# TensorE's work as a rolled loop, and GpSimd's drain in its own stream, in a gather, running-sum and projection kernel

## The chip, the cores and the metric

The kernel runs on one core of a Trainium2 chip. The metric is the device time of one execution in microseconds (us); five executions of the kernel before lay within 0.4% (356.56 to 357.88 us). A *run* below is one execution. The *span* is what the profile covers of the one execution it shows, and is 1.7 to 1.8 us shorter than that execution's time. Runs have a state: on the disturbed chip of two batches below the kernel before took 420 to 458 us at a granted TensorE clock of 0.88 to 0.98, where it takes 356 to 359 us at 0.99 on the others, and those are not compared with undisturbed ones. PSUM is the memory in which the kernel has TensorE write its products. The engines are TensorE (PE; PEld is its weight loads), VectorE (DVE), ScalarE (ACT), GpSimd (POOL) and SyncE (SP); a `q` behind the name is the engine's sequencer or queue.

## The reference, cut to what matters

```python
B, S, N, D = (16, 4096, 2048, 512)            # x: [B, S, D] f32, w: [D, D] f32, indices sorted
gathered = x[b_idx, indices, :]               # 2048 of 4096 rows of each batch
cs = np.cumsum(gathered, axis=1)              # running sum down the rows
return np.matmul(cs, w).astype(np.float32)    # [16, 2048, 512]
```

67 MB are read by gather and 67 MB written. There are 256 tiles of 128 rows, handled as 128 groups of two.

## The kernel before

The kernel gives each engine its own stream of instructions, and lets the streams meet in counting semaphores. `Lane.need` emits a wait only where that engine has not already waited for as much. These are the parts that the change and the argument touch:

```python
NG = 16; NH = 3; NA = 4; NB = 2; NC = 4; NO = 8; AH = 2     # buffers; AH groups of sums ahead
...
ctx.enter_context(tc.tile_critical(no_gpsimd_drain=False))  # L78: opens and closes the program
...
def gather(t):          # GpSimd: 128 rows of x by index, one DMA of 256 KB
    g, r = divmod(t, R)
    pool.need(s_c, g + 1 - NG // R)
    ...
    nc.gpsimd.indirect_dma_start(...).then_inc(s_g[t % NG], 16)   # 16 completions

def cast(g):            # ScalarE: both tiles of a group to fp16
    for t in range(R * g, R * g + R):
        act.need(s_g[t % NG], 16 * (t // NG + 1))
    act.need(s_a, R * (g - NH + 1))
    nc.scalar.copy(out=g16[g % NH][:], in_=g32[g % (NG // R)][:]).then_inc(s_c, 1)

def sums(t):            # TensorE: running sum inside a tile, with a triangular matrix
    g, r = divmod(t, R)
    pe.need(s_c, g + 1)
    pe.need(s_ut, 4)
    pe.need(s_d, t - NA + 1)
    for c in range(DC): mm = nc.tensor.matmul(out=pa[t % NA][:, c], ...)
    mm.then_inc(s_a, 1)

# carry(t): VectorE adds the last column of the tile before and writes fp16 into cst

def project(g, j):      # TensorE: running sums times w
    pe.need(s_wc, 1)
    pe.need(s_d, R * (g + 1))
    pe.need(s_e, g - NB + 1)
    for c in range(DC): mm = nc.tensor.matmul(out=pb[g % NB][:, j], ...)
    mm.then_inc(s_b, 1)

# drain(g): ScalarE copies pb to ob;  store(g): SyncE sends 512 KB to the output
...
for g in range(G):      # TensorE's order: sums of group g+2, then projection of group g
    for j in range(R):
        t = R * (g + AH) + j
        if t < T: sums(t)
        project(g, j)
```

"Drain" has two meanings here: `drain(g)` is ScalarE's copy out of PSUM, called the PSUM copy from here on. The other is the instruction DRAIN in GpSimd's stream, called the drain.

## Time and profile before

| | before |
|---|---|
| time, median of 3 runs | 357.12 us (356.56 to 357.59) |
| the profiled run, its span | 356.41 us, 354.6 us |
| gathers | 256, one each 1.25 us |
| bytes moved | 135.92 MB, mean 383 GB/s |

From the page of the kernel before come the busy times of the engines (share of the span, number of instructions), the queue that carries instruction blocks (packets, MB, share of the DMA engines' time), and the chain that ended last, by engine:

```profile
PE 301.8 (85%) x2050; PEld 149.2 (42%) x2050; DVE 178.1 (50%) x260; ACT 257.9 (73%) x258; POOL 243.7 (69%) x264
...
q8 instruction: 17, 0.28, 0.3%
...
POOL 50%; DMA 22%; issue 17%; PE 5%; ACT 3%; ACTq 0%; SPq 0%
```

TensorE is the busiest engine, but only 5% of the chain is its work. The gathers on GpSimd, the time between two of them ("issue") and the DMA behind them are 89%. So the 301.8 us of TensorE are mostly beside the path. In the same kernel, the view of the gathered tile gives the time from a gather's issue to its landing:

```profile
DMA to landing us min/median/max: 3.2/10.2/15.3
```

### The profile page before, as it was taken

Reading aid. Unit: us, or ns where it says so; the run is one execution under the profiler, and the core shown is the slowest. Engines: PE = TensorE matmul, PEld = TensorE weight load, DVE = VectorE, ACT = ScalarE, POOL = GpSimd, SP = SyncE. Lnnn points to the kernel's source line nnn. Section 1 sums busy time; section 2 is a strip of 40 time slices with the busy share of each in tenths; the row PEclk is TensorE's granted clock in tenths of the full one; section 3 lists DMA queues with packets and bytes.
Section 4 is the critical chain, followed back from the end, with each engine's and each line's share of the span. In section 5 each row is a group of like instructions: output and inputs, shape, how many; then the busy total and the mean of one; then the engine's idle time right before and its main releaser. Section 6 shows DMA issues by size and latency. Waiting matters only on the chain.

```text
span 354.6 us, 5833 instructions
## 1 busy us (share of the span) xinstructions
PE 301.8 (85%) x2050; PEld 149.2 (42%) x2050; DVE 178.1 (50%) x260; ACT 257.9 (73%) x258; POOL 243.7 (69%) x264
## 2 busy tenths in 40 slices
PE   0497799999899999899898988989989889898880
PEld 0253354444354444444444444444444444444440
DVE  1354465555555555555554554645555555555530
ACT  0776687787788787777777777877878778687760
POOL 6777777777777777777777777777777777774000
PEclk9999999999999999999999999999999999999995
DMA  6789999999999999999999999999999999999761
GB/s 222 224 241 384 409 410 401 415 411 418 412 417 416 415 414 415 413 416 416 415 415 414 414 413 413 411 417 415 413 417 413 416 413 414 412 415 414 293 244 74
DMA packets 40029, 135.92 MB, mean 383 GB/s; under 512 B 6465, under 2 KB 6721, under 8 KB 40001
## 3 DMA queue, kind: packets, MB, share of 16 engines
q0 software_dynamic: 20480, 67.13, 48.5%
q1 hardware_dynamic: 19520, 68.43, 47.8%
q8 instruction: 17, 0.28, 0.3%
q14 instruction: 12, 0.09, 0.1%
HBM read 68.42 MB, written 67.11 MB: 382 GB/s over the span
## 4 chain that ended last, share of the span: by engine, by line
POOL 50%; DMA 22%; issue 17%; PE 5%; ACT 3%; ACTq 0%; SPq 0%
POOL g L108 50%; DMA g<-in_x_dram,idxg 21%; PE pb L160 4%; ACT g L120 3%; PE pa L128 1%; ACT ob L172 1%; DMA idx_first<-in_indices_dram 1%; ACTq L23 0%; SPq L284 0%; SPq L78 0%
## 5 line engine op out<-in xcount | busy, mean ns | idle before, releaser
L108 POOL DMA_INDIRECT g<-in_x_dram,idxg x254 | 240.5, 947 | 77.4 <-issue 71.3
L160 PE MATMUL pb<-w,cst 128*128 128x512 f16 x1024 | 263.5, 381 | 0.0
L148 DVE TENSOR_TENSOR cst<-pa,cst 128x512 f16<-128x512 f32 x240 | 166.0, 692 | 138.1 <-PE pa L128 137.3
L120 ACT CAST g<-g 128x1024 f16<-128x1024 f32 x128 | 133.6, 1045 | 66.9 <-issue 32.2
L172 ACT COPY ob<-pb 128x1024 f32<-128x1024 f32 x128 | 129.2, 1010 | 11.4 <-PE pb L160 9.8
L128 PE MATMUL pa<-ut,g 128*128 128x128 f16 x1024 | 101.1, 222 | 38.5 <-ACT g L120 37.8
L128 PEld LDWEIGHTS pa<-ut,g 128*128 128x128 f16 x1024 | 69.4, 99 | 128.4 <-ACT g L120 97.6
L160 PEld LDWEIGHTS pb<-w,cst 128*128 128x128 f16 x1024 | 90.0, 98 | 62.0 <-issue 1.1
L143 DVE CAST cst<-pa 128x512 f16<-128x512 f32 x16 | 11.1, 692 | 20.4 <-PE pa L128 20.4
L120 ACT ACT_TABLE_LOAD x1 | 1.3, 1283 | 9.5 <-DMA g<-in_x_dram,idx_first 9.5
L229 PE MATMUL pb<-ident,idxf 128*128 128x128 f32 x2 | 0.9, 462 | 4.2 <-DVE idxf L225 4.2
L108 POOL DMA_INDIRECT g<-in_x_dram,idx_first x2 | 2.1, 1043 | 1.6 <-DMA idx_first<-in_indices_dram 1.3
L225 DVE CAST idxf<-idx 128x128 f32<-128x128 uint32 x2 | 0.5, 226 | 4.1 <-DMA idx<-in_indices_dram 4.1
L229 PEld LDWEIGHTS pb<-ident,idxf 128*128 128x128 f32 x2 | 0.4, 182 | 4.4 <-issue 4.2
L252 ACT CAST w<-w 128x2048 f16<-128x2048 f32 x1 | 1.9, 1892 | 0.0
L234 DVE CAST idxg<-pb 128x128 uint32<-128x128 f32 x2 | 0.6, 292 | 0.3
L198 POOL MEMSET ident<- 128x128 f32 x1 | 0.2, 205 | 0.5 <-SPq L78 0.5
L201 POOL TENSOR_SCALAR_AFFINE_SELECT ident<-ident 128x128 f32<-128x128 f32 x1 | 0.3, 288 | 0.1
L273 POOL MEMSET const-float32-0.0<- 128x1 f32 x1 | 0.1, 100 | 0.3 <-issue 0.3
L210 POOL TENSOR_SCALAR_AFFINE_SELECT ut<-ut 128x128 f16<-128x128 f16 x1 | 0.3, 292 | 0.0
L199 POOL MEMSET ut<- 128x128 f16 x1 | 0.2, 206 | 0.0
L273 POOL MEMSET const-uint8-127<- 128x1 uint8 x1 | 0.1, 117 | 0.0
(2 smaller groups left out, 0.2 us busy)
## 6 DMA issues: line engine op xcount, KB each, us to landing
out_dram<-ob SPq DMA_DIRECT2D x128, 512.0 KB, 7.2
g<-in_x_dram,idxg POOLq DMA_INDIRECT x254, 10.2
w<-in_w_dram SPq DMA_DIRECT2D x1, 1024.0 KB, 5.6
idx<-in_indices_dram SPq DMA_DIRECT2D x2, 128.0 KB, 2.3
g<-in_x_dram,idx_first POOLq DMA_INDIRECT x2, 5.1
idx_first<-in_indices_dram SPq DMA_DIRECT2D x1, 2.0 KB, 1.9
```

Source lines behind the costliest of these rows:

```text
L108: nc.gpsimd.indirect_dma_start(out=g32[g % (NG // R)][:, r, :], out_offset=None, in_=x_flat, in_offset=bass.IndirectOffsetOnAxis(ap=ap, ax ...
L120: nc.scalar.copy(out=g16[g % NH][:], in_=g32[g % (NG // R)][:]).then_inc(s_c, 1)
L128: mm = nc.tensor.matmul(out=pa[t % NA][:, c], lhsT=g16[g % NH][:, r, c * P : (c + 1) * P], rhs=ut[:], start=(c == 0), stop=(c == DC - 1),)
L143: nc.vector.tensor_copy(out=dst, in_=pa[t % NA][:]).then_inc(s_d, 1)
L148: nc.vector.tensor_tensor(out=dst, in0=pa[t % NA][:], in1=last.unsqueeze(2).broadcast_to([P, DC, R, Q]), op=mybir.AluOpType.add,).then_inc ...
L160: mm = nc.tensor.matmul(out=pb[g % NB][:, j], lhsT=cst[g % NC][:, c, j, :], rhs=w16[:, c, :], start=(c == 0), stop=(c == DC - 1),)
L172: nc.scalar.copy(out=ob[g % NO][:], in_=pb[g % NB][:]).then_inc(s_e, 1)
L201: nc.gpsimd.affine_select(out=ident[:], in_=ident[:], compare_op=mybir.AluOpType.is_equal, fill=0.0, base=0, pattern=[[-1, P]], channel_mu ...
L225: nc.vector.tensor_copy(out=idxf[:, k, :], in_=idx64[:, k, 0::2]).then_inc(s_if, 1)
L229: nc.tensor.transpose(out=pb[k % NB][:, 0, :P], in_=idxf[:, k, :], identity=ident[:]).then_inc(s_pt, 1)
L234: nc.vector.tensor_copy(out=idxg[:, k, :], in_=pb[k % NB][:, 0, :P]).then_inc(s_prep, 1)
L252: nc.scalar.copy(out=w16[:], in_=w32[:]).then_inc(s_wc, 1)
```

## The change

It is meant to shorten TensorE's stream (counted in the traces, from some 4,360 instructions to some 420 to be fetched): eight tiles (four groups) become the body of a loop, whose waits compare a semaphore with a register. The body needs constant buffer numbers, so the fp16 buffers go from three to four. In the body the projection of a group comes ahead of the sums two groups later. Apart from this, GpSimd's drain moves from the closing of the program into GpSimd's own stream, behind its last gather.

```diff
-    NH = 3
+    NH = 4
...
+    LOOP = 4
...
-    ctx.enter_context(tc.tile_critical(no_gpsimd_drain=False))
+    ctx.enter_context(tc.tile_critical(no_gpsimd_drain=True))
...
-    def sums(t):
+    def sums(t, first=0):
         g, r = divmod(t, R)
-        pe.need(s_c, g + 1)
-        pe.need(s_ut, 4)
-        pe.need(s_d, t - NA + 1)
+        if isinstance(first, int):
+            pe.need(s_c, g + 1)
+            pe.need(s_ut, 4)
+            pe.need(s_d, t - NA + 1)
+        elif r == 0:
+            nc.tensor.wait_ge(s_c, first + (g + 1))
...                               (project: the same, with two register waits where j == 0)
     for t in range(T):
         gather(t)
+    nc.gpsimd.drain()
...
+    def step(g, first=0):
+        for j in range(R):
+            project(g, j, first)
+            if not isinstance(first, int) or g + AH < G:
+                sums(R * (g + AH) + j, first)
...
-    for g in range(G):
-        for j in range(R):
-            t = R * (g + AH) + j
-            if t < T:
-                sums(t)
-            project(g, j)
+    for g in range(LOOP):
+        step(g)
+    with nc.tensor.Fori(LOOP, G - LOOP, LOOP) as first:
+        for g in range(LOOP):
+            step(g, first)
+    for g in range(G - LOOP, G):
+        step(g)
```

More of the change, by code (lines that the diff above doesn't have):

```diff
@@ L153, in carry, with project @@
         ).then_inc(s_d, 1)
-    def project(g, j):
-        pe.need(s_wc, 1)
-        pe.need(s_d, R * (g + 1))
-        pe.need(s_e, g - NB + 1)
+    def project(g, j, first=0):
+        if isinstance(first, int):
+            pe.need(s_wc, 1)
+            pe.need(s_d, R * (g + 1))
+            pe.need(s_e, g - NB + 1)
+        elif j == 0:
+            nc.tensor.wait_ge(s_d, R * first + R * (g + 1))
+            nc.tensor.wait_ge(s_e, first + (g - NB + 1))
         for c in range(DC):
```

## The prediction

> **What bounds the kernel now.** I read the page first, then the windows, the groups and waits, the last stretch of the timeline, and last the sequencer instructions of the source lines that open and close the program. From the page, the groups for gathers, projections and running sums:
>
> ```profile
> L108 POOL DMA_INDIRECT g<-in_x_dram,idxg x254 | 240.5, 947 | 77.4 <-issue 71.3
> L160 PE MATMUL pb<-w,cst 128*128 128x512 f16 x1024 | 263.5, 381 | 0.0
> L128 PE MATMUL pa<-ut,g 128*128 128x128 f16 x1024 | 101.1, 222 | 38.5 <-ACT g L120 37.8
> ```
>
> Columns: count, busy us, mean ns of one, idle us before them and what ended it. GpSimd issues a gather in 947 ns, with about 0.30 us between two, and waits for hardly anything else (the 20 waits put down to the casts last 0.3 us at most, the ordinary gap). In the timeline the gathers start every 1.25 us, the first at 3.25 us and the last at 322.66 us: 256 x 1.25 = 320 us. So gathers set the pace, 2.50 us for a group of two tiles. TensorE looks as busy (85%), but it has slack. In the timeline, where it had a backlog, its first sums of one group began at 21.68 us and of the next at 23.86 us: 2.18 us a group, 0.32 us under the gather's pace. The windows show that the 16 DMA engines are full behind the gathers:
>
> ```profile
> 45.00:110.00 65.00, 59.83 (x413) 29.62 (x412) 35.74 (x52) 51.22 (x53) 49.15 (x53) 1.00 1.03 412
> 250.00:300.00 50.00, 45.62 (x313) 22.32 (x311) 27.04 (x40) 38.74 (x40) 37.89 (x40) 1.00 1.03 415
> ```
>
> The last two columns are DMA share and GB/s. 256 KB read and 256 KB written each 1.25 us would be 419 GB/s; 412 to 415 move. So a backlog grows: a gather that took 8.2 us to land at 33 us takes 14.8 us at 323 us. The end is then read from the timeline:
>
> ```profile
> 322.66 0.95 POOL L108 DMA_INDIRECT g<-in_x_dram,idxg  x1 [0.30 <-issue]
> ...
> 337.56 1.04 ACT L120 CAST g<-g 128x1024 f16<-128x1024 f32 x1
> ...
> 340.06 4.48 PE L160 MATMUL pb<-w,cst 128*128 128x512 f16 x20
> ...
> 344.63 1.01 ACT L172 COPY ob<-pb 128x1024 f32<-128x1024 f32 x1 [0.71 <-PE pb L160]
> ```
>
> The last gather lands at 337.5 us, its cast follows at once, and TensorE then works off five tiles of projection without a gap, with three drains of PSUM that wait for it. The last store goes out at 345.67 us and lands at 348.3 us, yet the program ends at 354.6 us. What lies between stands under the source line that opens and closes the critical section, and in SyncE's own waits:
>
> ```profile
> L78 POOLq DRAIN  x1: 4965/4965/4965, 348.6 to 348.6; - x1
> L78 ACTq DRAIN  x1: 8/8/8, 348.6 to 348.6; - x1
> L78 DVEq DRAIN  x1: 17/17/17, 348.6 to 348.6; - x1
> ```
> ```profile
> SPq L78 <- POOLq L78: 4.8, 1, 4.8
> ```
>
> All engines drain at 348.6 us. The others take under 20 ns, GpSimd 4.97 us, and everybody waits. Nothing hides this time, and GpSimd had issued nothing for 25 us.
>
> [...]
>
> **The change, part by part.**
> *The drain.* It moves from the closing barrier into GpSimd's stream, behind its last gather at 323.6 us. Even if it has to wait there for all landings (337.5 us) and then runs 5 us it is over at 342.5 us, before the last store. The closing barrier keeps drains of under 20 ns. Off the path: SyncE's wait, 4.8 us.
> *Order of sums and projections.* Before, the projection of group g stood behind the sums of group g+2, and so behind that group's cast. Now half of it stands before them. In the steady state that buys nothing, since the gathers pace. At the end it does: after the last cast six tiles of projection were left (4 matmuls at 338.97 us and 20 after), now five. One tile is 4 x 0.215 us = 0.86 us, and the chain from there to the last drain is TensorE's. Off the path: 0.9 us.
> *Four buffers for NH instead of three.* Casts waited for sums 14 times, 8.6 us in all, in a stretch paced by landings. Worth nothing by itself; the loop needs a count that divides its four groups.
> *The loop.* 120 of 128 groups in 30 rounds of four. TensorE has 4 x 2.50 = 10.0 us for a round and needs 4 x 2.18 = 8.7: 1.3 us of slack. Added per round: some 24 register and wait instructions on the sequencer, which runs ahead of the array, and one branch. At [...]an estimated 0.05 us for each other instruction (the trace's semaphore instructions on TensorE take 0.051 us) that is about 1.3 us of sequencer time spread over 10 us, nearly all beside matmuls. On the path: 0.
> *Fetches.* 17 blocks of 16 KB become three or four if the loop stays resident. 14 blocks are 0.23 MB of 135.9 MB, 0.17%; with full DMA engines that is about 0.5 us of landing time at the end.
> Sum: 354.6 - 4.8 - 0.9 - 0.5 = 348.4 us span. The median time is 2.5 us above the profile's span (357.1 against 354.6), so 350.9 us; I say 351.0, 1.7% less.
>
> **Rivals.**
> 1. *The loop stalls on instruction fetch.* The body is 128 matrix instructions and some 26 others, about 154. Ahead of it stand about 180 TensorE instructions, so it runs from about 180 to 334[...]. If the sequencer drops a block as it enters the next, each of 29 branches back fetches its head anew. An estimate from the trace: 1.9 us, which the small index load took to land, plus 1.05 us of transfer, 3 us, less about 0.5 us that the sequencer is ahead. A round is then 8.7 + 2.5 = 11.2 us in place of 10.0, and 30 rounds add some 36 us: 387 us, TensorE the bound. For it: [...]one fetch for each block entered. Against it: [...]one who tunes would not keep this. I give it a quarter.
> 2. *Only the drain pays.* If the tail is set by landings and stores alone, 0.9 and 0.5 us fall away: 352.3 us. For it: the last landings slow with the full DMA engines, whatever TensorE does.
> 3. *The fetches were what made the backlog.* The growth of the landing time by 6.6 us would go with them: 351 - 6 = 345 us.[...] A tenth.
> 4. *The drain, among landing gathers, holds something up.* Nothing of GpSimd's follows it, so I give this little.
>
> **Range and chances.** The faster-by-2% line is 350.0 us, 1 us below my number: within the error of the small terms. Rival 3 and a luckier tail make 0.25. Rival 1 makes nearly all of slower, 0.22. The rest, 0.53, is within 2%. The range is 347.5 to 366: it holds the plain case and a mild stall (up to 0.5 us a round more than the slack), not the full one.
>
> **What will show it.** The closing GpSimd drain gone from the end and one of about 5 us at 323.6 us; 6.3 us from last landing to the end become 1.5. Gathers still every 1.25 us up to 322.7 us. The 16 KB instruction packets down to three or four. TensorE's 2.5 us per group without a gap at each eighth tile. After the last cast, 16 projection matmuls in place of 20 in the closing run. I am wrong if there is a gap of over 1 us in TensorE in each round, if instruction packets number 30 or more, or if the gathers start later than every 1.25 us because their buffers come free late.

Passages are cut from it where marked: statements on the fetching of instructions, on branches and on DMA engines that no trace or run shows. What the trace of the kernel before shows is this: 17 packets of 16,384 bytes ("blocks") for the 4,363 instructions of TensorE's stream, one for about 257, which took 0.89 to 1.43 us each; one compare-and-branch on TensorE's sequencer, of 174 ns; and no branch of a loop. The 1.3 us of sequencer time for a round counted a time for the branch; with 174 ns it is 24 x 0.05 + 0.17 = 1.4 us. That the sequencer runs ahead of the array is measured below, 0.9 to 1.1 us at the loop's branches; the 0.5 us of rival 1 was the author's estimate.

## The result, and the profile after

| | before | after |
|---|---|---|
| time, median | 357.12 us (356.56 to 357.88, 5 runs) | 351.19 us (350.75 to 351.56, 5 runs) |
| ratio of the fast runs | | 0.9834 (95%: 0.9817 to 0.9852) |
| the profiled run, its span | 356.41 us, 354.6 us | 351.22 us, 349.5 us |

A ratio here and below is the mean time of one kernel's fast runs over the mean of the other's fast runs of the same rounds on the same chip, so it is not quite the ratio of the medians that stand beside it. The gain is 1.7%, inside the 2% that counts as the same.

From the page of the kernel after, the lines that answer to those shown of before:

```profile
PE 299.2 (86%) x2050; PEld 149.7 (43%) x2050; DVE 178.2 (51%) x260; ACT 253.5 (73%) x258; POOL 243.7 (70%) x264
...
q8 instruction: 1, 0.02, 0.0%
...
POOL 47%; DMA 29%; issue 18%; ACT 3%; PE 1%; SPq 0%; ACTq 0%
...
L109 POOL DMA_INDIRECT g<-in_x_dram,idxg x254 | 240.5, 947 | 77.4 <-issue 69.8
L168 PE MATMUL pb<-w,cst 128*128 128x512 f16 x1024 | 263.5, 380 | 0.0
...
L132 PE MATMUL pa<-ut,g 128*128 128x128 f16 x1024 | 100.8, 222 | 40.4 <-ACT g L121 39.7
```

No engine does less than before: the matrix instructions are as many and take as long, and a gather still takes 947 ns. What is gone is 16 of 17 instruction packets. The chain is still that of the gathers (47 + 29 + 18 = 94%). The windows over the middle of the kernel after, with busy time and count by engine, clock, DMA share and GB/s, say the same:

```profile
45.00:110.00 65.00, 59.26 (x412) 29.58 (x411) 35.47 (x52) 50.09 (x52) 49.15 (x53) 1.00 1.03 415
250.00:300.00 50.00, 44.87 (x308) 22.05 (x305) 26.86 (x39) 38.17 (x40) 37.87 (x40) 1.00 1.02 411
```

As many gathers in each window as before (53 and 40), at 415 and 411 GB/s in place of 412 and 415. So nothing changed in the steady state, and the difference must lie at the end. The timeline of the kernel after, from the last gather on (start, duration, engine, line, operation, idle time before it and what ended it):

```profile
322.62 0.95 POOL L109 DMA_INDIRECT g<-in_x_dram,idxg  x1 [0.31 <-issue]
...
338.14 1.04 ACT L121 CAST g<-g 128x1024 f16<-128x1024 f32 x1 [0.73 <-issue]
...
340.56 3.62 PE L168 MATMUL pb<-w,cst 128*128 128x512 f16 x16
...
344.26 1.01 ACT L180 COPY ob<-pb 128x1024 f32<-128x1024 f32 x1 [0.71 <-PE pb L168]
```

Together with the stores and the end of the trace this gives the place of every microsecond:

| us from the start of the span | before | after |
|---|---|---|
| last gather issued | 322.66 | 322.62 |
| last cast starts | 337.56 | 338.14 |
| last PSUM copy starts | 344.63 | 344.26 |
| last store issued | 345.67 | 345.30 |
| last store landed | 348.27 | 347.93 |
| end | 354.60 | 349.51 |

Three differences make up the 5.1 us. From the last landing to the end there are 1.58 us in place of 6.33: 4.75 won. From the last cast to the last PSUM copy there are 6.12 us in place of 7.07: 0.95 won, with 16 projection matmuls in the closing run where there were 20. But the last cast itself comes 0.58 us later. The rest, 0.03 us, is a last store that took as much longer to land.

Where the drain went is shown in the kernel after by its source line in GpSimd's stream (line 229, duration in ns, start), and by that of the closing section (line 79):

```profile
L229 POOLq DRAIN  x1: 21955/21955/21955, 318.6 to 318.6; - x1
```
```profile
L79 ACTq DRAIN  x1: 8/8/8, 348.2 to 348.2; - x1
L79 POOLq NOP  x1: 13/13/13, 348.2 to 348.2; - x1
```

The moved drain's record begins at 318.6 us, when the last four gathers have yet to start, and ends at 318.6 + 21.96 = 340.6 us, 7.6 us ahead of the closing barrier. There GpSimd now has an instruction of 13 ns. The drain waits for the landings: in the six undisturbed traces that have it moved, its end lies 2.4 us after the start of the last cast (340.56 - 338.14 here, 339.54 - 337.11 in `loop16`, further down), though that start differs by up to 2.1 us between them. After the last landing (338.07 us) it took 2.5 us, half of the 4.97 it takes at the end. For the loop, the view of its source line on TensorE's sequencer (count, min/median/max in ns, first and last start in us):

```profile
L259 PEldq FUSED_REGOPS  x30: 44/44/44, 23.3 to 324.2; - x30
L259 PEldq COMPARE_BRANCH  x30: 76/208/223, 36.4 to 334.0; - x30
```

30 rounds, 29 branches taken at 207 to 223 ns and the last, not taken, at 76. The sequencer runs ahead: each branch is over 0.9 to 1.1 us before the array comes to the next round. In the timeline after one of these branches (at 106.23 us) the array loses nothing between the sums that end one round and the projection that begins the next:

```profile
107.18 0.39 PE L132 MATMUL pa<-ut,g 128*128 128x128 f16 x4
107.41 1.03 PE L168 MATMUL pb<-w,cst 128*128 128x512 f16 x4
```

The projection starts 0.16 us before the (modelled) end of the sums. So it does at the end of all 30 rounds, and in `unrolled_b`, the same kernel without a loop, at the same places. Finally, the landing times of the kernel after:

```profile
DMA to landing us min/median/max: 3.5/9.4/15.4
```

The slowest landing is 15.4 us as it was 15.3. After, it is the last gather's, which lands at 338.07 us; before, the last gather took 14.8 us and landed at 337.49. That is the 0.58 us of the last cast.

### The profile page after: what moved, and what is told of

The parts are those of the page before. It is cut to its first block, busy times and chain, and to the rows that moved or that the text cites. A ratio compares the mean times of both kernels' runs of the same rounds, so it can differ in the third digit from the quotient of the medians.

```text
span 349.5 us, 6009 instructions
## 1 busy us (share of the span) xinstructions
PE 299.2 (86%) x2050; PEld 149.7 (43%) x2050; DVE 178.2 (51%) x260; ACT 253.5 (73%) x258; POOL 243.7 (70%) x264
## 4 chain that ended last, share of the span: by engine, by line
POOL 47%; DMA 29%; issue 18%; ACT 3%; PE 1%; SPq 0%; ACTq 0%
POOL g L109 47%; DMA g<-in_x_dram,idxg 29%; ACT g L121 3%; PE pb L168 1%; DMA idx_first<-in_indices_dram 1%; ACT ob L180 0%; PE pa L132 0%; SPq L300 0%; ACTq L23 0%; SPq L79 0%
```

## The experiments

The theory after the result: the drain pays 4.8 us, the order of sums and projections 0.9 us, and neither the loop nor the saved fetches (of instruction blocks) pay or cost anything that can be told from the spread of the last landing. The rivals: (a) it is all the drain, and the tail's 0.9 us is chance; (b) the loop costs something that the saved fetches pay back; (c) the drain's 5 us are not tied to the gathers, and a drain merely has to stand somewhere; (d) the loop is free of fetches only because its body is short.

### A first batch, on a disturbed chip

Four kernels: the drain alone, everything but the drain's move, the change without the rolled loop, and the order alone.

`drain_only`:

```diff
-    ctx.enter_context(tc.tile_critical(no_gpsimd_drain=False))
+    ctx.enter_context(tc.tile_critical(no_gpsimd_drain=True))
...
         gather(t)
+    nc.gpsimd.drain()
```

> The kernel before with the closing GpSimd drain moved behind the last gather, nothing else. My theory: this is nearly the whole gain, 4.8 us, so about 352.3 us, with a drain in GpSimd's stream that starts when the last gathers are issued and ends only after the last of them has landed (the changed kernel's took 22 us, to 340.6 us), and 1.5 us from the last store's landing to the end. Rival (the rolled loop and its missing instruction fetches bring a good part): a gain under 3.5 us, over 353.6 us.

`loop_only` (against the kernel after):

```diff
-    ctx.enter_context(tc.tile_critical(no_gpsimd_drain=True))
+    ctx.enter_context(tc.tile_critical(no_gpsimd_drain=False))
...
-    nc.gpsimd.drain()
```

> The changed kernel with the drain put back at the end: the loop, the order of sums and projections and the fourth buffer alone. My theory: 0.4 to 0.9 us faster than before, 356.2 to 356.7 us, with a closing GpSimd drain of 5 us. Rival (missing fetches bring the gain): 355 us or less.

`unrolled` (against the kernel after):

```diff
-    with nc.tensor.Fori(LOOP, G - LOOP, LOOP) as first:
-        for g in range(LOOP):
-            step(g, first)
+    for g in range(LOOP, G - LOOP):
+        step(g)
```

> The changed kernel with its loop written out, so that order, buffers and drain stay and only the loop goes. My theory: within 0.5 us of the changed kernel, about 351.2 us, though the 17 instruction packets of 16 KB come back[...]. Rival 1 (the fetches cost landing time): 352 us or more. Rival 2 (branches and register waits cost): 350.5 us or less.

`order_only` (against the kernel before):

```diff
             t = R * (g + AH) + j
+            project(g, j)
             if t < T:
                 sums(t)
-            project(g, j)
```

> The kernel before with projection and sums exchanged in TensorE's stream and nothing else. My theory: five tiles of projection after the last cast become the work of one tile less, 0.9 us off, 356.2 us. Rival (only landings and stores set the tail): 357.1 us, no change.

Measured: the kernel before itself took 420.37 to 457.96 us in these rounds. The medians were 439.0 (`drain_only`), 460.66 (`loop_only`), 457.96 (`unrolled`) and 461.54 (`order_only`). What goes with this level stands in the page of `drain_only`, GB/s in 40 slices of the span:

```profile
GB/s 231 211 209 196 299 331 328 349 328 324 350 325 344 345 322 328 337 352 330 333 332 353 310 337 343 289 343 327 291 327 335 315 307 347 351 335 341 343 236 211
```

Between the first and last four slices it moves 289 to 353 GB/s, where the kernel before moved 401 to 418 on an undisturbed chip, at a granted clock of 0.921. What held the transfers back is not shown. Here a few microseconds can't be measured in the times, and by these none of the expectations was met or refuted. One thing is told as a caution. The three kernels with the projection ahead of the sums were slower than the kernel before in the same rounds (ratios 1.0632, 1.0672 and 1.0831, of two or three fast runs each, with intervals up to 0.076 wide, a verdict of unclear), and `drain_only`, with one fast run and no ratio, was not. The fast runs of these three had a clock of 0.89 to 0.92, those of the kernel before 0.97 to 0.98. I have no explanation that was tested.

Two parts of the change can still be read from the ends of these traces. From the last landing to the end there are 6.3 us in `loop_only` and `order_only`, which close with GpSimd's drain, and 1.6 us in `drain_only` and `unrolled`, which do not. So without its move the drain stays where it was, whatever the loop, order and buffers. `loop_only`:

```profile
L79 POOLq DRAIN  x1: 4965/4965/4965, 458.3 to 458.3; - x1
```

And in `order_only`, which has three buffers and no loop, the closing run of projections has 16 matmuls, so this is the work of the order alone:

```profile
444.56 3.62 PE L160 MATMUL pb<-w,cst 128*128 128x512 f16 x16
```

Here it won nothing, though: from the last cast to the last PSUM copy there are 7.1 us in `order_only` and 7.0 in `drain_only`. TensorE was behind, with 28 projection matmuls left after that cast in both. By these traces the order pays where TensorE keeps up with the casts, and not where it is behind.

### The drain alone, and the change without the loop, on an undisturbed chip

`drain_only_b` and `unrolled_b` are the same two kernels as above, again.

> The same kernel as drain_only, again, since that batch ran on a chip in a disturbed state (before took 420 to 458 us there, in place of 357). My theory: the moved drain alone brings 4.8 us, so 352.3 us where before takes 357.1 us. Rival (the rolled loop and its missing instruction fetches bring a good part): a gain under 3.5 us.

> The same kernel as unrolled, again, for the same reason. My theory: within 0.5 us of the changed kernel's 351.2 us, though the 17 instruction packets of 16 KB come back. Rival 1 (the fetches cost landing time): 352 us or more. Rival 2 (branches and register waits cost): 350.5 us or less.

Measured, beside 357.01 us for the kernel before (9 runs): `drain_only_b` 352.0 us (351.36 to 352.71, 4 runs), ratio 0.9854 (0.9837 to 0.9871); `unrolled_b` 350.61 us (349.98 to 351.31, 5 runs), ratio 0.9819 (0.9802 to 0.9836). The timelines of their ends, `drain_only_b` first:

```profile
338.36 1.04 ACT L120 CAST g<-g 128x1024 f16<-128x1024 f32 x1 [0.64 <-issue]
...
340.78 4.48 PE L160 MATMUL pb<-w,cst 128*128 128x512 f16 x20
...
345.35 1.01 ACT L172 COPY ob<-pb 128x1024 f32<-128x1024 f32 x1 [0.71 <-PE pb L160]
```
```profile
337.64 1.04 ACT L121 CAST g<-g 128x1024 f16<-128x1024 f32 x1 [0.79 <-issue]
...
340.06 3.62 PE L168 MATMUL pb<-w,cst 128*128 128x512 f16 x16
...
343.76 1.01 ACT L180 COPY ob<-pb 128x1024 f32<-128x1024 f32 x1 [0.71 <-PE pb L168]
```

The drain's move alone wins 357.01 - 352.0 = 5.0 us. From the last cast to the last PSUM copy it is 345.35 - 338.36 = 6.99 us with the old order and 343.76 - 337.64 = 6.12 us with the new one, as in the kernel after, where the loop is rolled. In all six undisturbed traces with the new order it is 6.12 to 6.13 us. So the tail's 0.87 us belongs to the order of TensorE's stream and not to the loop, and rival (a) falls. The medians of the two kernels lie 1.4 us apart, the two profiled runs 2.0 us: beside the 0.87 us, the last gather landed 0.7 us earlier in the one than in the other, and the last store took 0.4 us less.

The page of `unrolled_b` for the instruction queue:

```profile
q8 instruction: 16, 0.26, 0.3%
```

It has the fetches back. Its median, 0.58 us under the 351.19 of the kernel after, lies just outside the 0.5 us expected and just above the 350.5 of the expectation's second rival (branches cost), so it decides less than was hoped. Its ratio (0.9819) is not above that of the kernel after (0.9834); the intervals overlap. So the rolled loop shows no gain. Nor is a cost shown: if the difference is one, it is 0.0015 x 357 = 0.5 us. Rival (b), a cost and a repayment of several microseconds, would need the two to be equal by accident, and there is no gap at the branches in which a cost could lie.

### The drain left out

`no_drain` (against the kernel after): nobody drains GpSimd inside the program.

```diff
         gather(t)
-    nc.gpsimd.drain()
```

> The changed kernel without the drain in GpSimd's stream. My theory: the 5 us belong to the first drain after gathers, wherever it stands, so the drain that the end of the program holds anyway takes 5 us in place of 0.04 us and the kernel takes about 356 us. Rival (the 5 us belong to the critical section's own drain): 351 us.

Measured: 355.63 us, one run of unknown state (the kernel before: 357.77, 7 runs, same chip). The drains that close the whole program, behind the critical section, in the view of their source line:

```profile
L299 POOLq DRAIN  x3: 40/122/4965, 348.0 to 353.7; - x3
```

The first of these takes 4.965 us, from 348.03 us on; in the kernel after the same one takes 0.041 us. So the 5 us belong to the first drain after the gathers, here at the program's end (4.965 us) as in the kernel before at the critical section's (4.965 us), and not to the one that the change removed: leaving out that drain only handed the cost to the next. Later drains of GpSimd take 0.03 to 0.12 us in both. A drain of GpSimd ahead of the gathers is short: the one at 0.4 us in the kernel before takes 0.19 us. Rival (c) falls. The gain comes from the place alone, behind the last gather, where 15 us of landings and 6 us of TensorE's tail cover it. What the 5 us are spent on is not shown.

### Longer loop bodies

`loop16` and `loop32` (against the kernel after):

```diff
-    LOOP = 4
+    LOOP = 16        (loop32: 32)
```

> The changed kernel with 16 groups in a round in place of four, so a loop body of some 570 TensorE instructions[...], run 6 times. My theory ([...]the loop stays resident): as many 16 KB instruction packets as the program has blocks, about 6, no gap at the branch back, 351 us. Rival[...]: two or three packets more for each round, 15 to 20 in all, and a gap of about 3 us in TensorE at each branch.

> The same with 32 groups in a round: a body of some 1140 instructions, four to five blocks, run twice. [...]12 to 13 packets and no gap at the one branch back. If it keeps fewer than five: 16 to 18 packets and a gap of about 3 us there. The time can't tell (one gap of 3 us is taken up by the slack), the packets do.

Measured: 350.2 and 350.53 us, one run each, of unknown state. Bodies of 562 and about 1,120 TensorE instructions, so at 257 for a packet some 2.2 and 4.4 packets' worth, with 6 and 2 rounds. From the pages and the views of the loop's line, `loop16` first, then `loop32`:

```profile
q8 instruction: 6, 0.10, 0.1%
...
L259 PEldq COMPARE_BRANCH  x6: 76/208/223, 97.4 to 302.3; - x6
```
```profile
q8 instruction: 12, 0.20, 0.2%
```

In `loop16` no instruction packet moves between 88.6 and 312.2 us, the stretch of the five branches back, and in `loop32` none between 165.4 and 266.3 us, which holds its one branch back at 178.5 us. Both numbers of packets are what the straight length of the stream needs, about one for each 257 instructions after the first. So a body of about 1,120 instructions was run again without a new packet, and rival (d) falls up to that size. The time does not depend on the body's length within the spread of single runs.

### The slowest completion

A gather sets 16 completions, and the cast needs them all. The author's argument tied each of them to a DMA engine; the traces don't name the engines, so this was not shown. The slowest of the 16 comes 6.6 to 7.4 us after the median one in the kernel before, late in the run, and 7.0 to 7.7 us after it in the kernel after (from the packed trace: means over the 11th to 15th gather of each of the 16 gather semaphores, those with lost records left out). If that completion came sooner, so would the last landing. `split16` cuts 8 of 128 stores into 120 and 8 partitions, meant to take load off the one DMA engine held to be slow. Which engines a store uses is shown by no run here, and the 345 to 347 us were the author's estimate.

```diff
         sp.need(s_e, g + 1)
+        if SPLIT(g):                            (SPLIT(g): g % 16 == 13)
+            nc.sync.dma_start(out=dst[:120], in_=ob[g % NO][:120]).then_inc(s_o[g % NO], 16)
+            nc.sync.dma_start(out=dst[120:], in_=ob[g % NO][120:]).then_inc(s_o[g % NO], 16)
+            return
...                               (waits on s_o count 32 for such a store)
```

> The changed kernel with 8 of its 128 stores cut in two: 120 partitions[...] and 8 partitions[...]. It asks why the last gather lands 15 us after its issue when the median of its 16 completions comes after 6 us. My theory: [...]the last cast starts at 331 to 333 us in place of 338 us, and the kernel takes 345 to 347 us. Rival[...]: last cast at 338 us, 351 us, no change.

Measured: 352.15 us (351.64 to 352.39, 4 runs), ratio 0.9844 (0.9809 to 0.988), no better than the kernel after. The landing times of the gathers in `split16`:

```profile
DMA to landing us min/median/max: 3.6/10.5/16.4
```

No relief; the slowest landing is 16.4 us. The engines of a store are not seen, so what the split did to the load of any of them is not shown either. What holds the slowest completion back stays open.

### A last batch, disturbed again

`after_b` is the kernel after once more. `ahead1` is `drain_only` with one group of sums ahead in place of two and the last PSUM copy in halves, an attempt to shorten the tail further:

```diff
-    AH = 2
+    AH = 1
...
+        if g == G - 1:
+            act.need(s_b, R * g + 1)
+            nc.scalar.copy(out=ob[g % NO][:, 0], in_=pb[g % NB][:, 0]).then_inc(s_e0, 1)
...                               (then the second half; the last store waits for both)
```

> The changed kernel itself, unaltered, so that the last experiment is compared on one chip in the same rounds. 351.2 us where before takes 357.1 us, ratio 0.983 to 0.984.

> The kernel before (written out, old order, three buffers) with the moved drain, sums and casts one group ahead of the projections in place of two, and the last group's copy out of PSUM in two halves. My theory: time from the last cast on is TensorE's and is set by how many projection tiles are left: four, in place of six before and five in the changed kernel, and half a copy less. From the start of the last cast to the start of the last whole copy it was 7.0 us with six and 6.1 us with five; with four 5.3 us, and 0.5 us off for the half copy. So 352.0 - 1.7 - 0.5 = 349.8 us, about 1 us below the changed kernel. Rival (one group ahead is too little, TensorE waits for the running sums in each group, 0.3 us of slack is used up): over 353 us, gathers later than every 1.25 us.

Measured: these fell on the chip of the first batch. The kernel before took 422.89 to 454.12 us, `after_b` 454.99 (ratio 1.0666, 1.0577 to 1.0756, unclear by its verdict), `ahead1` 465.32 (one fast run of 444.07, no ratio). The comparison that was wanted is not to be had from this. But the caution of the first batch stands firmer: on this disturbed chip the kernel after was slower than the kernel before, and so, by their medians, were all kernels tried there that do not keep the old order with two groups ahead. This is told, not explained. In the trace of `ahead1` the closing run has 12 projection matmuls, and from the last cast to the last PSUM copy there are 5.3 us, where `drain_only` had 7.0 on that chip, so its tail is shorter there. Whether `ahead1` beats both kernels on an undisturbed chip stays open, and no version tried is shown to beat the kernel after: `unrolled_b` (350.61 us), `loop16` (350.2) and `loop32` (350.53) came out 0.6 to 1.0 us under its median, but the first has an overlapping interval and the other two are single runs.

## Why the prediction was right or wrong

The prediction held: 351.0 us predicted, 351.19 measured, inside "the same". Step by step:

- **The drain, 4.8 us.** Right: 4.75 us in the traces and 5.0 us by `drain_only_b`. That a drain of about 5 us would stand behind the last gather was not seen so: the record is one of 21.96 us from 318.6 us on, as it includes the wait for the landings. Its end, put at 342.5 us at the worst, was 340.6: the wait was there, but 2.5 us and not 5 remained after the last landing.
- **Order of sums and projections, 0.9 us.** Right: 0.95 us in the kernel after, 0.87 us between `drain_only_b` and `unrolled_b`, with 16 matmuls in place of 20, as foretold. It was not timed by itself in a clean run, as `order_only` fell on the disturbed chip and `unrolled_b` also has the fourth buffer; but the trace of `order_only` has the 16 matmuls with three buffers.
- **Four buffers, 0.** Consistent: the casts' waits for sums are gone (8.6 us in 14 waits before, none after), and neither the gathers' pace nor the last landing moved with them. It was not tried alone.
- **The loop, 0.** Right within what can be told, 0.5 us. The counts were rough: the body is 142 instructions where 154 were estimated, as only 14 of them are not matrix instructions, and it begins at about the 174th instruction where 180 were estimated (164 matrix instructions, and 9 others, stand ahead of it). A branch taken costs 208 ns of the sequencer (median), and the array does not notice it: the projection behind it starts 0.16 us before the end of the sums.
- **Fetches, 0.5 us.** This is the term that failed. The packets fell to 1, further than the three or four foretold, but the last cast came 0.6 us later and not 0.5 us earlier. The completions show why nothing was won. Between the slowest of a gather's 16 and the second slowest lie 3.6 to 4.0 us in the kernel before, but 6.2 to 6.9 us in the kernel after, while the slowest keeps its distance to the median. `unrolled_b`, with 16 packets, has 2.9 to 3.7 us and `drain_only_b`, with 17, 3.3 to 4.1; `loop16` and `loop32`, with 6 and 12, have 4.8 to 5.5; `no_drain` and `split16`, with one, 6.1 to 7.2. The completions next after it move too, less and less, to about the seventh slowest (distance from the median in the kernel before and in the kernel after: 3.2 and 0.8 us for the second slowest, 0.7 and 0.1 for the seventh). So in these eight traces, with more packets several completions came later, the second slowest by some 3 us, but not the one that every landing waits for. The step took "full DMA engines" as one pool of bytes, where the last of 16 completions decides. The 0.6 us the other way is no cost of the change that I could show: the last cast starts between 337.1 and 339.2 us in the eight undisturbed traces, in no order with packets or loop.
- **The offset from span to time, 2.5 us.** Also mis-sized. It was the median of some runs less the span of another, faster one. The profiled run itself took 356.41 us, so the offset is 1.8 us, and 1.7 after. The span was predicted 1.1 us too short (348.4 against 349.5) and the offset 0.8 us too long, and the two nearly cancelled. The total is therefore better than its parts.
- **Rival 1, a stall on instruction fetch (387 us).** Wrong, though the loop does run over from one block into the next: its first instruction is about the 174th and its last about the 315th, where a packet brings about 257, and the only 16 KB packet, at 28.7 us, falls inside the first round (23.3 to 36.4 us). 29 branches back follow it without another packet, so nothing of the body was fetched anew. The quarter given to this was too much.
- **Rival 2, only the drain (352.3 us).** `drain_only_b` came to 352.0 us, but the tail of the kernel after is the shorter one that this rival denied.
- **Rival 3, fetches made the backlog (345 us).** Wrong: with one packet left, the slowest landing is 15.4 us.
- **Rival 4.** Nothing was held up by the moved drain; the last store landed 2.6 us after its issue in both kernels.

## What to carry to other kernels

Look at what each engine does between the last landing and the end: a wait that only one engine needs may be able to run in that engine's own stream while others still work, as it did here (5.0 us won by `drain_only_b`), but leaving it out may only hand it to the next barrier (4.965 us again in `no_drain`). Where the stream of an engine is not what sets the pace, a shorter one bought nothing here, and the saved bytes bought nothing, as the slowest of the completions that a landing waits for kept its distance to the median (6.6 to 7.4 us with 17 packets, 7.0 to 7.7 with one). When adding an offset to a profiled span, take it from the profiled run itself.
